# Moving the expert stage's residual sums and the last gate conversions in a one-core transformer block

## The chip, the cores and the metric

The kernel runs on one core of one Trainium2 chip. The metric is device time in microseconds (us) of one execution. Four compute engines work from queues of their own: PE (TensorE: matrix products, with PEld as its weight loads), DVE (VectorE), ACT (ScalarE) and POOL (GpSimd); SP issues most of the DMA transfers. An instruction runs when those ahead of it in its engine's queue have run and the semaphores that it waits for have come.

## The reference, cut to what matters

All tensors are float32; there are 1024 tokens of 1024 channels, 32 experts, four experts per token.

```python
h = layer_norm(DEEPNORM_ALPHA * h + mix, ln1_g, ln1_b)         # first half of the block: attention, gating
logits = h @ w_router + b_router                               # top 4 of 32 experts per token
gate = min(xb @ w_gate + b_gate, 7); up = clip(xb @ w_up + b_up, -7, 7)
y = ((up + 1) * gate * sigmoid(1.702 * gate)) @ w_down + b_down    # per expert, for its tokens
h = layer_norm(DEEPNORM_ALPHA * h + sum_of_gated_y, ln2_g, ln2_b)
ple = (p @ w_ple) * sigmoid(h @ w_ple_gate + b_ple_gate)
out = layer_norm(DEEPNORM_ALPHA * h + ple, ln3_g, ln3_b)
```

## The kernel before, in words

Precision is kept with pairs of float16: a float32 weight or activation is split into a high part (an ACT copy, scaled) and a low part (a DVE scalar_tensor_tensor that subtracts the high part), and a product takes three matmuls (high by high, high by low, low by high). A piece of weight of 512 rows by 512 columns is a "unit". `stage` loads it (1 MB, SP queue), `high(n)` makes its high part on ACT and `low(n)` its low part on DVE; `convert(n)` is both.

The instructions of each engine are issued in the order in which the Python program writes them (`tc.manual_schedule()`). Small `Pipe` objects delay work by a number of ticks: `p.at(2, f)` runs f two ticks later, so the place of a `tick` or a `drain` decides where in each queue an instruction stands. Operations that a pipe runs directly carry the line of `Pipe.tick`, L63.

The expert stage (`moe`) walks through `seq`, a list of steps numbered n, one unit each. Per expert (r, in the order ORDER) these are eight steps for the gate and up products ("g" and "u") and four for the down product ("d"). At step n the program runs `high(n + 4)`, then `low(n + 3)`, then the step's matmuls. For the first expert, steps 0 to 7 are the g and u products, steps 8 to 11 the d product; this expert is one of three in FULL, whose down weights are not split but used as float32 straight from the stage, so those four units have no conversion. Step 12 begins the second expert (window 96 tokens), step 20 the third (window 232).

Around this stand four things that the change touches:

- The tiles' sums. `start(i)` in `mid` (L888) multiplies tile i's gates by the 32 down biases (two matmuls, L895, into two PSUM banks of the eight that all of PE's work shares), adds ALPHA times the residual (two DVE operations on 128x512, L63, one tick later) and writes the 512 KB tile to `acc` in device memory (POOL queue, two ticks later). There are eight tiles. `step()` (L990) ticks mid's pipe and starts one tile; it is called at the end of each step n below 14 (L1534), so that the tiles start at steps 0 to 7. Expert results are later added to `acc` by indirect transfers (L1379), whose order behind those writes is kept.
- `find(2, pipe)` (L1525), at step 4: a one-hot mask on DVE (eight operations, L1240) for the third expert; two ticks later PE picks the tokens (L1248), and a tick after that POOL gathers their rows (L1267).
- The gate of the last part, `w_ple_gate`, is four units, converted as numbers len(seq) to len(seq)+3. The first is converted within the last d product, the second right after the steps (L1542), ahead of a hardware loop over overflowing tokens (`For_i`, L1548), the last two behind it in `more()` (L1595). Of the 16 `ple_tile` products (six matmuls each, evicted by ACT), eight are before the loop and eight behind it. With these inputs the loop is passed without a turn.
- The last part (`post`): three tiles of `acc` are loaded, `more()` runs, tile 0 is normalised on DVE and transposed by `turn` (PE, then a split on ACT and DVE), and tile 1 is normalised. Then the loop over eight tiles runs `gate(i, 0)`, which ends in a matmul with the bias row `k.bg` (L1697; the row is split by `fill_bg`, on ACT and DVE), `turn(i + 1)` and `gate(i, 1)`. `gate(i, 0)` reads units 0 and 1, `gate(i, 1)` units 2 and 3.

Of the kernel before, what the change touches and what calls it, by code (L numbers as in the profile page):

```python
# [205 lines left out]
def three(nc, ps, n, lhs, rhs):  # L206

    for b in range(n):
        (lh, ll), (rh, rl) = lhs(b), rhs(b)
        nc.tensor.matmul(ps, lh, rh, start=b == 0, stop=False)  # L210
        nc.tensor.matmul(ps, lh, rl, start=False, stop=False)  # L211
        nc.tensor.matmul(ps, ll, rh, start=False, stop=b == n - 1)  # L212
# [19 lines left out]
def pair(t, *sl):  # L232
    return lambda b: tuple(t[(slice(None), s, b, *sl)] for s in range(2))
# [908 lines left out]
def moe(k, windows, m, p):  # L1142
# [5 lines left out]
    R = len(windows)  # L1148
# [6 lines left out]
    pipe = Pipe()  # L1155
# [22 lines left out]
    seq = []  # L1178
# [14 lines left out]
    staged, units, seen = {}, {}, set()  # L1193
# [12 lines left out]
    def high(n):  # L1206
        if n < len(loads):
            if loads[n][0] == "p" or loads[n][0] == "d" and full(loads[n][1]):
                units[loads[n]] = staged.pop(n)
                return  # L1210
            units[loads[n]] = k.t8([P, 2, KB // 2, 512], F16, "unit")
            nc.scalar.activation(units[loads[n]][:, 0], staged[n], AF.Copy, scale=WS)  # L1212

    def low(n, part=None):

        if 0 <= n < len(loads):
            if n in staged:
                u = units[loads[n]]
                sl = slice(0, 4) if part is None else slice(2 * part, 2 * part + 2)
                nc.vector.scalar_tensor_tensor(u[:, 1, sl], staged[n][:, sl], WS, u[:, 0, sl], op0=OP.mult, op1=OP.subtract)  # L1220
                if part == 0:
                    return
                del staged[n]
            stage(n + N_AHEAD)

    def convert(n):
        high(n)
        low(n)
# [42 lines left out]
    def find(r, p, soon=False):  # L1271

        if r >= R:
            return
        oh = onehot(r, lambda b: k.place[:, b, r:r + 1])

        def second():
            ts = pick(r, oh, lambda b: k.val[:, b, :, r])
            if soon:
                gather(r, ts)  # L1280
            else:
                p.at(1, gather, r, ts)
        p.at(1 if soon else 2, second)

    def turn(r, w0, n, h, p):

        if r not in xgT:
            xgT[r] = k.t8([P, 2, KB, 256], F16, "xgT")
        t, x = xgT[r], xg[r, w0]
        pt = k.bank()  # L1290
        for j in range(4):
            b = 4 * h + j
            nc.tensor.transpose(pt[:, j * P:j * P + n], x[:n, b * P:(b + 1) * P], k.identf[:n, :n])
        src = pt.rearrange("p (j t) -> p j t", j=4)[:, :, :n]
        hi, lo = (t[:, s, 4 * h:4 * h + 4, w0:w0 + n] for s in range(2))

        def fin():
            nc.scalar.activation(hi, src, AF.Copy, scale=16.0)  # L1298
            nc.vector.scalar_tensor_tensor(lo, src, 16.0, hi, op0=OP.mult, op1=OP.subtract)  # L1299
        p.at(1, fin)  # L1300
# [26 lines left out]
    def s1(kind, r, u, p):  # L1327
        un = units.pop((kind, r, u))
        banks = chunks(kind, r, u)
        columns(r, u, un, xgT[r], banks)  # L1330
        if u % 2:
            p.at(1, take, kind, r, u // 2, banks, p)
# [98 lines left out]
    def ple_turns():  # L1431
        st = units.pop(("p", R, 0)).rearrange("p a (b c) -> p (a b) c", b=2)
        ple["p"] = k.t8([P, 2, 2, T], F16, "pT")
        for i in range(0, NB, 2):
            pt = k.bank()
            for j in range(4):
                nc.tensor.transpose(pt[:, j * P:(j + 1) * P], st[:, i + j // 2, (j % 2) * P:(j % 2 + 1) * P], k.identf)
            pt = pt.rearrange("p (i k t) -> p k i t", i=2, k=2)
            sl = slice(i * P, (i + 2) * P)
            hi, lo = (ple["p"][:, s, :, sl].rearrange("p k (i t) -> p k i t", i=2) for s in range(2))  # L1440

            def fin(hi=hi, lo=lo, pt=pt):
                for kk in range(2):
                    k.split(hi[:, kk], lo[:, kk], pt[:, kk], 16.0)
            pipe.at(1, fin)

    def ple_tile(i, h):
        if i % 2 == 0 and h == 0:
            ple[i] = k.t8([P, 2, D], FT, "ple")
            k.pl += [ple[i][:, 0], ple[i][:, 1]]  # L1450
        ps = k.bank()
        u = units["x", R, 0]
        three(nc, ps, 2, pair(ple["p"], slice(i * P, (i + 1) * P)), lambda b: tuple(u[:, s, 2 * b + h] for s in range(2)))
        pipe.at(1, nc.scalar.activation, k.pl[i][:, h * 512:(h + 1) * 512], ps, AF.Copy, 0.0, 1.0 / (16.0 * WS))

    k.pl = []
    ple_tiles = [(i, h) for i in range(NB) for h in range(2)]
# [27 lines left out]
    for n, (kind, r, u) in enumerate(seq):  # L1485
        pipe.tick()
        if n + LEAD < len(seq):
            high(n + LEAD)
        if n == 2:
            low(4)  # L1490
        if n > 1 and n + LEAD - 1 < len(seq):
            low(n + LEAD - 1)
        elif n == 0:
            low(2)
        if n >= 30:
            next(over, None)
        if n == len(seq) - 8:
            fill_bg = post_rows(k)
        if kind == "p":
            ple_turns()  # L1500
        elif kind == "d":
            if (r, u) == (R - 1, 1):
                for _ in range(2):
                    ple_tile(*ple_tiles.pop(0))
            if r in (0, R - 1) and u == 1:
                pipe.drain()
            if (r, u) == (R - 1, 1):
                convert(len(seq))
            s2(r, u, pipe)
            if r == 0 and u in (1, 3):  # L1510
                turn(1, 0, windows[1], u // 2, pipe)
        elif kind != "x":
            s1(kind, r, u, pipe)
            if n == 0:
                rest, turns, step, biases = next(m)
            if n == 1:
                biases("g", 0)
                turns()
                find(1, pipe, True)
                gather(0, pick(0, oh, val), False)  # L1520
                over = rest()
                low(3)
            if n in (3, 5, 7):
                biases(kind, u // 2)
            if n == 4:  # L1525
                find(2, pipe)
            if r and (kind, u) == ("g", 2):
                find(r + 2, pipe)
            if r and u >= 2 and r + 1 < R:
                i = 2 * (kind == "u") + u - 2  # L1530
                ws = win(r + 1)
                if i % 2 < len(ws):
                    turn(r + 1, *ws[i % 2], i // 2, pipe)
        if n < 14:  # L1534
            step()
        if n == 14:
            p.drain()
    for _ in range(3):
        pipe.tick()
        for _ in range(2):  # L1540
            ple_tile(*ple_tiles.pop(0))
    convert(len(seq) + 1)  # L1542
    pipe.drain()


# [1 line left out]
    n = nc.values_load(k.n_over[0:1, 0:1], min_val=0, max_val=N_OVER)  # L1547
# [43 lines left out]
    us = []  # L1591

    def more():

        for n in range(2, 4):  # L1595
            convert(len(seq) + n)
        us.extend(units.pop(("w", R, u)) for u in range(4))
        fill_bg()
        for n, t in enumerate(ple_tiles):
            ple_tile(*t)  # L1600
            if n % 2:
                pipe.tick()
        pipe.drain()
        del units["x", R, 0]
    return us, more


LEAD, N_AHEAD, N_FIRST = 4, 6, (4, 8)
# [3 lines left out]
def post_rows(k):  # L1612

    k.bg, fill = row_halves(k, k.a["b_ple_gate"], "bg")
    k.rows = {}
    for n in ("ln2_g", "ln2_b", "ln3_g", "ln3_b"):
        k.rows[n] = k.t4([P, D], FT, n)
        k.row(k.rows[n], k.a[n][0])
    return fill


def post(k, us, more, p):
# [10 lines left out]
    su, me, sq, va, y, t = (k.small([P, 2], FT, f"pn{c}", 1) for c in range(6))  # L1633
# [42 lines left out]
    def turn(i, h):  # L1676
        if h == 0:
            hs[i] = k.t4([P, 2, KB, P], F16, "h2T")
        pt = k.bank()
        for j in range(4):  # L1680
            b = 4 * h + j
            nc.tensor.transpose(pt[:, j * P:(j + 1) * P], h2[i][:, b * P:(b + 1) * P], k.identf)
        pt = pt.rearrange("p (j t) -> p j t", j=4)
        k.split(hs[i][:, 0, 4 * h:4 * h + 4], hs[i][:, 1, 4 * h:4 * h + 4], pt, 4.0)
# [24 lines left out]
    load(0)  # L1709
    load(1)  # L1710
    load(2)
    more()
    for i in range(2):
        k.norm(h2[i], D, rows["ln2_g"], rows["ln2_b"], EPS * AS * AS, None, 1 if i else 2)
        if i == 0:
            for h in range(2):
                turn(i, h)
    fin, done = None, {}

    def finish(i):  # L1720
# [76 lines left out]
```

## Time and profile before

| | us |
|---|---|
| three timed runs | 2163.43, 2163.64, 2168.16 (median 2163.64) |
| the profiled execution | 2162.48 |
| its span, first to last instruction | 2160.8 |
| PE, DVE, ACT busy | 2088.8, 1665.1, 1332.7 |

The profile has one execution. Besides totals it has timelines (start and duration of each instruction, and in brackets the idle time of the engine before it with what ended that), waits (who waited for whom) and windows (busy time by engine in a stretch, with the clock that TensorE was granted as a share of full speed). A PE matmul's duration is longer than its pitch, since matmuls are pipelined. Times below are counted from the span's start.

### The profile page before, as it was taken

Reading aid. Unit: us, or ns where it says so; the run is one execution under the profiler, and the core shown is the slowest. Engines: PE = TensorE matmul, PEld = TensorE weight load, DVE = VectorE, ACT = ScalarE, POOL = GpSimd, SP = SyncE. Lnnn points to the kernel's source line nnn. Section 1 sums busy time; section 2 is a strip of 40 time slices with the busy share of each in tenths; the row PEclk is TensorE's granted clock in tenths of the full one; section 3 lists DMA queues with packets and bytes.
Section 4 is the critical chain, followed back from the end, with each engine's and each line's share of the span. In section 5 each row is a group of like instructions: output and inputs, shape, how many; then the busy total and the mean of one; then the engine's idle time right before and its main releaser. Section 6 shows DMA issues by size and latency. Waiting matters only on the chain. (4 is left out here: it accounts for less than half of the span.)

```text
span 2160.8 us, 54807 instructions
## 1 busy us (share of the span) xinstructions
PE 2088.8 (97%) x23236; PEld 1695.0 (78%) x23236; DVE 1665.1 (77%) x2807; ACT 1332.7 (62%) x1925; POOL 262.4 (12%) x272
## 2 busy tenths in 40 slices
PE   7999889999999999999999999999999999999897
PEld 6797556544469879889889898999999989999443
DVE  4677666523256888969788899999889998998688
ACT  3324555412110357778778788888878888888642
POOL 1000000000100020111102121221312122221100
PEclk9999999999999999999999999999999999999999
DMA  7201211412132598999989999999999999999611
GB/s 249 70 21 31 72 51 56 127 45 63 50 113 79 220 340 307 347 354 355 368 301 336 347 361 375 364 347 366 354 319 367 359 361 346 363 348 377 212 49 59
DMA packets 278603, 520.14 MB, mean 241 GB/s; under 512 B 12092, under 2 KB 61292, under 8 KB 278320
## 3 DMA queue, kind: packets, MB, share of 16 engines
q1 hardware_dynamic: 262688, 464.10, 59.7%
q0 software_dynamic: 15664, 52.47, 9.0%
q8 instruction: 185, 3.03, 0.6%
q14 instruction: 66, 0.54, 0.1%
HBM read 476.93 MB, written 33.30 MB: 236 GB/s over the span
## 5 line engine op out<-in xcount | busy, mean ns | idle before, releaser
L1220 DVE SCALAR_TENSOR_TENSOR unit<-stage,unit 128x2048 f16<-128x2048 f32 (+1 forms) x378 | 856.8, 2278 | 73.3 <-ACT unit L1212 72.5
L1324 PE MATMUL bank<-xgT,unit 128*128 128x120 f16 (+22 forms) x4096 | 754.5, 226 | 1.2 <-DVE xgT L1299 1.2
L1323 PE MATMUL bank<-xgT,unit 128*128 128x120 f16 (+22 forms) x4096 | 754.7, 226 | 1.0 <-ACT z L1342 1.0
L1325 PE MATMUL bank<-xgT,unit 128*128 128x120 f16 (+22 forms) x4096 | 754.4, 226 | 0.7 <-DVE unit L1220 0.7
L1212 ACT ACTIVATE unit<-stage 128x2048 f16<-128x2048 f32 x377 | 717.0, 1912 | 49.3 <-DVE unit L1220 25.3
L1324 PEld LDWEIGHTS <-unit 128*128 128x128 f16 x5056 | 496.3, 98 | 7.1 <-issue 1.9
L1323 PEld LDWEIGHTS <-unit 128*128 128x128 f16 x5056 | 496.6, 98 | 6.2 <-issue 1.3
L1325 PEld LDWEIGHTS <-unit 128*128 128x128 f16 x5056 | 496.3, 98 | 4.8 <-issue 1.4
L1342 ACT ACTIVATE z<-bank,bias 128x120 f32<-128x120 f32 (+22 forms) x512 | 156.5, 379 | 88.3 <-PE bank L1325 87.8
L1323 PE MATMUL bank<-hT,unit 128*128 128x232 f16 (+14 forms) x960 | 207.8, 238 | 0.0
L1325 PE MATMUL bank<-hT,unit 128*128 128x232 f16 (+14 forms) x960 | 207.8, 238 | 0.0
L1324 PE MATMUL bank<-hT,unit 128*128 128x232 f16 (+14 forms) x960 | 207.8, 238 | 0.0
L1379 POOL DMA_INDIRECT acc_dram<-y,slot_i x47 | 117.3, 2495 | 527.8 <-ACT y L1376 523.8
L1267 POOL DMA_INDIRECT xg<-h_dram,slot_i x46 | 108.3, 2355 | 599.8 <-DVE slot_g L1262 314.3
L224 PE MATMUL bank<-xT,unit 128*128 128x512 f16 x384 | 145.5, 379 | 2.7 <-DVE pT L63 2.7
L226 PE MATMUL bank<-xT,unit 128*128 128x512 f16 x384 | 145.5, 379 | 1.6 <-DVE unit L105 1.6
L225 PE MATMUL bank<-xT,unit 128*128 128x512 f16 x384 | 145.5, 379 | 0.0
L210 PE MATMUL bank<-unit,xT 128*128 128x256 f16 (+1 forms) x384 | 106.2, 277 | 2.3 <-ACT unit L104 2.3
L211 PE MATMUL bank<-unit,xT 128*128 128x256 f16 (+1 forms) x384 | 106.0, 276 | 2.1 <-DVE unit L105 2.1
L212 PE MATMUL bank<-unit,xT 128*128 128x256 f16 (+1 forms) x384 | 106.0, 276 | 0.0
L105 DVE SCALAR_TENSOR_TENSOR unit<-stage,unit 128x1024 f16<-128x1024 f32 (+2 forms) x37 | 60.1, 1657 | 58.7 <-ACT unit L104 58.6
L1299 DVE SCALAR_TENSOR_TENSOR xgT<-bank,xgT 128x512 f16<-128x512 f32 (+7 forms) x92 | 50.7, 552 | 56.8 <-ACT xgT L1298 56.3
(392 smaller groups left out, 3499.1 us busy)
## 6 DMA issues: line engine op xcount, KB each, us to landing
stage<-in_w_gate_up_dram SPq DMA_DIRECT2D x256, 1024.0 KB, 9.7
stage<-in_w_down_dram SPq DMA_DIRECT2D x128, 1024.0 KB, 9.6
stage<-in_w_in_dram SPq DMA_DIRECT2D x22, 512.0 KB, 4.2
stack<-qk_tmp SPq DMA_DIRECT2D x96, 64.0 KB, 2.0
stage<-in_w_in_dram SPq DMA_DIRECT2D x5, 1024.0 KB, 11.3
xs<-in_x_dram SPq DMA_DIRECT2D x8, 512.0 KB, 12.2
crow<-c_dram SPq DMA_DIRECT2D x8, 512.0 KB, 4.5
stage<-in_w_out_dram SPq DMA_DIRECT2D x4, 1024.0 KB, 6.2
```

The lines of the kernel that those rows point to most:

```text
L210: nc.tensor.matmul(ps, lh, rh, start=b == 0, stop=False)
L224: nc.tensor.matmul(box[0], lh, rh, start=b == 0, stop=False)
L225: nc.tensor.matmul(box[0], lh, rl, start=False, stop=False)
L226: nc.tensor.matmul(box[0], ll, rh, start=False, stop=b == n - 1)
L1212: nc.scalar.activation(units[loads[n]][:, 0], staged[n], AF.Copy, scale=WS)
L1220: nc.vector.scalar_tensor_tensor(u[:, 1, sl], staged[n][:, sl], WS, u[:, 0, sl], op0=OP.mult, op1=OP.subtract)
L1267: nc.gpsimd.indirect_dma_start(out=x[:n], out_offset=None, in_=k.h1d, in_offset=bass.IndirectOffsetOnAxis(ap=i[:n, :1], axis=0))
L1323: nc.tensor.matmul(o, wh, x[:, 0, kb, :W], start=start, stop=False, skip_group_check=True)
L1324: nc.tensor.matmul(o, wh, x[:, 1, kb, :W], start=False, stop=False, skip_group_check=True)
L1325: nc.tensor.matmul(o, wl, x[:, 0, kb, :W], start=False, stop=stop, skip_group_check=True)
L1342: nc.scalar.activation(zs[r][c // 2][:, k0 + c % 2, :W], banks[c // n][:, c % n, :W], AF.Identity, bias=bias_of(r, 4 * v + c + 4 * k0), sc ...
L1379: st = nc.gpsimd.indirect_dma_start(out=k.acc, out_offset=bass.IndirectOffsetOnAxis(ap=idx[r, w0][:n, :1], axis=0), in_=y[:n], in_offset=N ...
```

## The change

The tiles' sums are started two per step in steps 8 to 11, and mid's pipe is drained at step 11 in place of step 14; `find(2)` stands at step 6 in place of step 4. The second gate unit is converted behind the loop in place of ahead of it. `more` becomes a generator of two parts: the first converts the second unit and runs the eight remaining `ple_tile`s (a tick after each, in place of after two); the second converts the last two units and the bias row. The first part is called where `more()` was, the second after tile 0 was normalised and transposed.

```diff
-            if n == 4:
+            if n == 6:
                 find(2, pipe)
...
-        if n < 14:
+        if 8 <= n < 12:
             step()
-        if n == 14:
+            step()
+        if n == 11:
             p.drain()
...
-    convert(len(seq) + 1)
     pipe.drain()
...
     def more():

+        convert(len(seq) + 1)
+        for t in ple_tiles:
+            ple_tile(*t)
+            pipe.tick()
+        pipe.drain()
+        del units["x", R, 0]
+        yield
         for n in range(2, 4):
             convert(len(seq) + n)
         us.extend(units.pop(("w", R, u)) for u in range(4))
         fill_bg()
-        for n, t in enumerate(ple_tiles):
-            ple_tile(*t)
-            if n % 2:
-                pipe.tick()
-        pipe.drain()
-        del units["x", R, 0]
-    return us, more
+        yield
+    return us, more()
...
-    more()
+    next(more)
     for i in range(2):
         k.norm(h2[i], D, rows["ln2_g"], rows["ln2_b"], EPS * AS * AS, None, 1 if i else 2)
         if i == 0:
             for h in range(2):
                 turn(i, h)
+            next(more)
```

## Rows read from the trace of the kernel before

**Rows 1.** The page: busy time, share of the span and instructions of each engine.
```profile
PE 2088.8 (97%) x23236; PEld 1695.0 (78%) x23236; DVE 1665.1 (77%) x2807; ACT 1332.7 (62%) x1925; POOL 262.4 (12%) x272
```
**Rows 2.** Windows, steps 1-7, 8-11, 12-20: busy us by engine, granted clock, DMA share, GB/s.
```profile
755.70:788.50 32.80, 30.23 (x421) 27.21 (x419) 27.52 (x61) 12.39 (x24) 11.01 (x10) 0.90 0.86 313
788.50:804.70 16.20, 16.20 (x77) 7.87 (x76) 10.88 (x14) 11.55 (x15) 1.20 (x3) 1.00 1.04 386
804.70:828.20 23.50, 22.38 (x427) 21.99 (x424) 23.40 (x33) 22.80 (x35) 2.15 (x2) 1.00 1.05 381
```
**Rows 3.** Groups by line, DVE, 755.7 to 788.5: busy us, mean ns, idle.
```profile
L63 DVE SCALAR_TENSOR_TENSOR h<-h,bank 128x512 f32<-128x512 f32 x14 | 8.9, 677 | 0.0
```
**Rows 4.** Timeline of DVE, steps 2 to 15.
```profile
765.10 4.48 DVE L1220 SCALAR_TENSOR_TENSOR unit<-stage,unit 128x2048 f16<-128x2048 f32 x2
...
788.55 1.28 DVE L63 SCALAR_TENSOR_TENSOR h<-h,bank 128x512 f32<-128x512 f32 x2 [2.78 <-PE bank L895]
...
794.64 2.28 DVE L1220 SCALAR_TENSOR_TENSOR unit<-stage,unit 128x2048 f16<-128x2048 f32 x1
796.84 0.40 DVE L1361 SCALAR_TENSOR_TENSOR hT<-sig,z 128x240 f32<-128x240 f32 x1
...
804.68 11.09 DVE L1220 SCALAR_TENSOR_TENSOR unit<-stage,unit 128x2048 f16<-128x2048 f32 x5
```
**Rows 5.** Waits of PE, 750 to 810: who for whom, us, times, longest.
```profile
PE bank L1248 <- DVE z L1359: 1.1, 1, 1.1
PE bank L1323 <- ACT z L1342: 1.0, 1, 1.0
...
PE bank L895 <- DVE h L63: 0.5, 1, 0.5
```
**Rows 6.** Windows of steps 4 and 5 alone (48 matmuls of a unit in each).
```profile
769.50:773.70 4.20, 4.20 (x49) 4.14 (x48) 4.20 (x6) 1.55 (x2) 2.08 (x3) 0.59 1.05 409
774.00:776.60 2.60, 2.60 (x50) 2.50 (x48) 2.60 (x4) 0.00 (x0) 0.53 (x1) 1.00 0.99 255
```
**Rows 7.** Tile view, steps 8 to 11: ns min/median/max, first and last start.
```profile
L1401 PE MATMUL bank<-stage,hT x32: 590/592/690, 788.6 to 802.5; 128*120 128x512 f32 x32
```
**Rows 8.** Timeline of DVE behind the loop.
```profile
2034.77 4.49 DVE L1220 SCALAR_TENSOR_TENSOR unit<-stage,unit 128x2048 f16<-128x2048 f32 x2
2039.28 1.22 DVE L701 SCALAR_TENSOR_TENSOR bg<-brow,bg 1x1024 f16<-1x1024 f32 x1
...
2052.36 1.29 DVE L105 SCALAR_TENSOR_TENSOR h2T<-bank,h2T 128x512 f16<-128x512 f32 x2 [5.17 <-ACT h2T L104]
2053.56 1.27 DVE L148 BATCH_NORM_STATS2 bn_s<-h 128x6 f32<-128x512 f32 x2
```
**Rows 9.** Timeline of ACT behind the loop.
```profile
2032.83 3.71 ACT L1212 ACTIVATE unit<-stage 128x2048 f16<-128x2048 f32 x2 [1.73 <-DVEq L1548]
...
2051.73 1.08 ACT L104 ACTIVATE h2T<-bank 128x512 f16<-128x512 f32 x2
```
**Rows 10.** Timeline of PE behind the loop.
```profile
2035.71 0.61 PE L210 MATMUL bank<-unit,pT 128*128 128x512 f16 x1 [5.44 <-DMA h<-acc_dram]
...
2039.83 0.58 PE L210 MATMUL bank<-unit,pT 128*128 128x512 f16 x1 [2.65 <-issue]
...
2057.86 0.38 PE L1697 MATMUL bank<-bg,sel 128*128 128x512 f16 x1
2059.91 1.09 PE L1682 MATMUL bank<-identf,h 128*128 128x128 f32 x8 [1.67 <-DVE pn L1645]
```
**Rows 11.** Line L1548 (the loop), 2015 to 2045: ns min/median/max, first and last start.
```profile
L1548 PEldq COMPARE_BRANCH  x3: 97/192/3594, 2028.2 to 2035.5; - x3
```
**Rows 12.** Waits of SP's queue, 2022 to 2110.
```profile
SPq L1548 <- DVEq L1548: 1.6, 1, 1.6
```
**Rows 13.** Windows behind the loop and in the last part.
```profile
2039.80:2042.90 3.10, 3.07 (x8) 1.12 (x8) 2.91 (x8) 0.60 (x1) 0.00 (x0) 0.50 0.49 197
2043.10:2051.00 7.90, 7.90 (x38) 3.62 (x37) 3.85 (x9) 3.58 (x6) 0.00 (x0) 1.00 0.00 0
...
2071.80:2139.00 67.20, 67.20 (x336) 33.41 (x335) 60.73 (x164) 29.54 (x54) 2.79 (x5) 1.00 0.15 55
```

## The prediction

> **What bounds the kernel now.** The page's totals come first: PE is busy for 97% of the span, DVE for 77% [rows 1]. Those are averages, so I read windows next, around the two places that the diff touches. In steps 1 to 7 (755.7 to 788.5) DVE has 27.5 of 32.8 us and PE's granted clock averages 0.90; in steps 8 to 11 PE is never idle and DVE has 10.9 of 16.2; from 804.7 to 828.2 DVE has 23.4 of 23.5 [rows 2]. So in this order the bound is DVE, then PE on float32 matmuls, then DVE. Behind the loop the chain of waits runs along PE: PE restarts at 2035.71, runs the eight remaining `ple_tile`s, and DVE waits 5.17 us for it before the split of tile 0 at 2052.36 [rows 8, 10]. In the last part PE is busy throughout (67.20 of 67.20 us) [rows 13], so what delays PE there delays the end.
>
> **Steps 0 to 7 get shorter.** 14 DVE operations of the sums, 8.9 us, lie in 755.7 to 788.5 [rows 3]; the last of the eight pairs is the one at 788.55, 1.28 us [rows 4]. All eight move. On PE that takes away:
> - the waits of 1.1, 1.0 and 0.5 us [rows 5], 2.6 us in all. I put them down to banks: two per tile, held until DVE, which lags, has read them, out of eight.
> - two slow steps. Step 4, behind the 1.0 us wait, ran at a granted clock of 0.59 (between the levels 1.2 and 2.4 GHz) and took 4.2 us; step 5, at 1.00, took 2.6 [rows 6]. Step 6, behind the 1.1 us wait, is like step 4. 2 x 1.6 = 3.2 us.
> - 16 matmuls (L895) at a pitch of 0.22 us: 3.5 us. The pitch is that of a 512-column matmul, 7.90 us by 38 at full clock, 0.21 [rows 13].
> - the pick of `find(2)`, 16 small matmuls, taken as 0.7 us (between nothing and the 1.1 us of the wait ahead of it); it comes back in step 8, so its size cancels.
>
> That is 10.0 us. About 0.9 of it comes back, because PE then catches up with DVE's low part of unit 3. Step 8 starts some 9 us earlier: 788.6 becomes 779.5. The conversions have room for that: two low parts take 4.48 us, from 765.10 [rows 4], with 3.7 us of sums gone ahead of the last of them.
>
> **Steps 8 to 11 take it back.** PE: 16 float32 products in 32 passes from 788.6 to 803.1 with half a microsecond of transposes between [rows 7], so 3.5 us per step, plus 0.9 for two tiles, plus 0.7 once. That alone would be 19 us, to 798.5. DVE doesn't let it. Its queue at step 8 holds the first pair of sums, which waits for the first tile's matmuls, which PE issues behind the step's own: 779.5 + 0.7 + 3.5 + 0.4 = 784.1. Until then DVE is idle and everything else queues behind. From there it has the 10.9 us of today less today's last pair (1.2), eight pairs at 8.9/7 = 1.27, and a microsecond for `find(2)`'s slots: 20.9, of which successive operations overlap by a tenth or two each, so about 20 us [rows 2 to 4]. PE's third float32 unit (step 10) needs the last hT. DVE reaches it after: first pair 1.2, slots and glu 1.4, low part 2.2, two pairs 2.4, glu 1.0, low part 2.2, hT 0.4: 794.9. Today the same hT runs at 796.84, when step 8 began at 788.6 [rows 4, 7]: it ended 8.7 us behind step 8's start and will end 15.4 behind it. PE wants it for step 10 at 788.8 and stands for some 4 us; 1.0 us was enough for a fall of the clock [rows 6], so I charge another 1.6. DVE in turn waits for tile 4's matmuls (1.4 us, and the 1.6 of the slow clock). The second expert's five low parts, which start at 804.68 [rows 4], then start at 784.1 + 20 + 1.4 = 805.5 without the clock's fall and at 807.1 with it. DVE has no slack from there to 828 [rows 2], so this passes on: +0.8 or +2.4 us. I take +2.4, since the shorter wait of rows 5 already cost it, and keep +0.8; at most 4.7 us could be gained (PE's 798.5 against 803.2).
>
> The queues in passing: POOL's eight writes to `acc` (512 KB each) go from steps 2 to 8 to steps 9 to 12, and the first indirect add waits for their landing; behind it in POOL's queue stands only the gather for the fourth expert, which step 16 asks for. SP's weight loads keep their order; the 4 MB of writes fall in a stretch in which the DMA share is 1.04 as well as 0.86 before it [rows 2], so loads up to step 17 come earlier and those after at the same time. I cost both at nothing; the cover is the order of megabytes, not spare rate, and if loads come late it costs up to 2 us. `find(2)`'s gather comes two steps later for a transpose at step 16: nothing.
>
> **Behind the loop.** The second unit's conversion leaves the place ahead of the loop. SP waited 1.6 us there for DVE [rows 12], so SP, ACT and DVE pass the loop up to 1.5 us earlier. PE does not: its branch took 3.594 us [rows 11], begun just after its last matmul, which the 5.44 us of idle put at 2030.3 [rows 10], and the restart at 2035.71 follows from that. The waits name the load of `acc` as the releaser of that restart [rows 10]; by them PE would start 1.5 us earlier too. The Trainium skill (Runtime: NRT & Kernel Launch, Instruction fetch mechanics) says that a taken branch to code outside the fetched window stalls until that code is fetched. By that rule the restart stays; by the waits the total below would be 1.5 us less.
>
> The unit itself, 1.9 us on ACT and 2.2 on DVE (half of the pairs of 3.71 and 4.49) [rows 8, 9], is hidden by PE's restart and `ple_tile`s, which end at 2051.0; the cover is over 9 us. The ticks change nothing, as ACT follows PE tile by tile.
>
> The last two units and the bias row ran in that same cover. Now they stand behind tile 0's split in both queues. ACT ends the split at 2052.8 (2051.73 + 1.08) [rows 9]; its first high part is there at 2054.6. DVE has then 4.49 + 1.22 [rows 8]: 2060.3, where before it went on at 2053.56 with tile 1's statistics [rows 8]. From those to the transposes of tile 1 at 2059.91 [rows 10] is 6.35 us. So the transposes start at 2066.65: +6.7 us. PE, which waited 1.67 us there [rows 10], has nothing else: `gate(0, 0)` ends in the bias row's matmul (2057.86 [rows 10]), now held to 2060.3, then 6.3 us of idle. After an idle time of 5.44 us PE ran at a granted clock of 0.50 [rows 10, 13]; half of 3.1 us is 1.6 lost. Between nothing and 2 us, I take 1.6.
>
> **Sum.** +2.4 + 6.7 + 1.6 = +10.7 us on the profiled execution's 2162.5: 2173.2. The median of the runs shown is 1.2 us above that execution, within its spread. Forecast: 2173 us, about 0.45% slower; its own range is 2170 to 2177 (head from 0 to +4, clock from 0 to 2).
>
> **Rivals.** About 0.3%, 6.5 us, is what can be told from no change: below 2157.1 is faster, above 2170.1 slower.
> 1. The head's gain stays (0.17). DVE keeps up in steps 8 to 11, and PE's own 19 us decide: -4.7 + 8.3 = +3.6, 2166 us, within. For it: DVE is a third idle there today. Against: the first pair is held behind the step's matmuls.
> 2. The other side, not slower: the last two conversions don't stand behind tile 0's split (0.08). Place: DVE's and ACT's queues between 2042 and 2052, where DVE has 10 us of idle. If low parts start before the split there, both tail terms go: +2.4, 2165 us, within; it decides once they start before 2051. Against: DVE stood 5.17 us before that split with tile 1's statistics behind it [rows 8], so its queue isn't reordered.
> 3. Both 1 and 2, with the 1.5 us of the loop (0.09): 2162.5 - 4.7 - 1.5 = 2156, faster.
> 4. The change doesn't do in steps 0 to 7 what it says (0.16): the waits of rows 5 come from ACT's and DVE's reads of other tiles and stay with their slow steps, 2 x (1.0 + 1.6) = 5.2, while four tiles' banks in each of steps 8 to 11 make new ones: 2178 us, slower.
>
> The forecast itself has 0.50. Slower: 0.50 + 0.16 + 0.04 of 1 = 0.70. Within: 0.13 of 1 + 0.08 of 2 = 0.21. Faster: 0.09. The range 2165 to 2179 leaves out rival 3 and the far end of 4.
>
> **What would show it.** Right: step 8 starting near 780; DVE idle until the first sums near 784; a PE stall of 3 to 5 us ahead of the third float32 unit; the second expert's low parts starting 0 to 3 us later than 804.68. Behind the loop PE restarting at the same distance from its last matmul, DVE's two low parts behind the split of tile 0, and an idle time of some 6 us ahead of tile 1's transposes with a half-clock stretch after it. Wrong: transposes of tile 1 within 2 us of today's place counted from PE's restart, or steps 12 on starting 3 us earlier.

## The result, and the profile after

The changed kernel takes 2176.32 us (median of 6 runs, 2173.99 to 2177.88) where the kernel before takes 2164.10 beside it: ratio 1.0052, 95% interval 1.0040 to 1.0064. It is slower by 12.2 us by the medians and by 11.3 by the ratio (8.7 to 13.9); 2173 was forecast, and the time lies in the range.

The page of the changed kernel, busy time by engine, hardly differs from [rows 1]: PE's busy time has grown by 5.9 us with the same number of matmuls, so some of them took longer; the rows below show some at half clock.

```profile
PE 2094.7 (96%) x23236; PEld 1697.0 (78%) x23236; DVE 1665.0 (77%) x2807; ACT 1333.3 (61%) x1925; POOL 271.3 (12%) x272
```

**A zero for the comparison.** Two profiled executions are not aligned before the changed code begins: the DVE operation at L910, just ahead of step 0, starts at 748.40 before and at 749.95 after. Places in the expert stage are therefore counted from that operation, places behind the loop from PE's restart there. A time "on the scale of before" is one of the changed kernel less those 1.55 us.

**The expert stage.** Windows of steps 1 to 7, 8 to 11 and 12 to 20 of the changed kernel (columns as in [rows 2]):

```profile
757.30:781.70 24.40, 24.03 (x382) 23.19 (x378) 18.03 (x39) 12.07 (x23) 9.72 (x1) 0.93 0.85 296
781.70:808.80 27.10, 22.90 (x123) 11.20 (x123) 20.28 (x36) 14.07 (x17) 7.11 (x10) 0.94 0.98 354
808.80:832.40 23.60, 22.25 (x408) 21.56 (x408) 23.50 (x33) 20.74 (x34) 3.26 (x4) 1.00 1.04 368
```

The first stretch shrank from 32.8 to 24.4 us. The second grew from 16.2 to 27.1, and in it PE, never idle before, is idle for 4.2. DVE shows why (timeline of the changed kernel; in brackets the idle time ahead and its releaser):

```profile
776.92 0.40 DVE L1361 SCALAR_TENSOR_TENSOR hT<-sig,z 128x240 f32<-128x240 f32 x1
782.18 0.16 DVE L1250 COPY slot_t<-bank 128x4 f32<-128x4 f32 x1 [4.86 <-PE bank L1248]
...
786.33 1.29 DVE L63 SCALAR_TENSOR_TENSOR h<-h,bank 128x512 f32<-128x512 f32 x2 [3.59 <-PE bank L895]
...
794.38 0.40 DVE L1361 SCALAR_TENSOR_TENSOR hT<-sig,z 128x240 f32<-128x240 f32 x1
...
796.90 0.40 DVE L1361 SCALAR_TENSOR_TENSOR hT<-sig,z 128x240 f32<-128x240 f32 x1
...
800.87 1.28 DVE L63 SCALAR_TENSOR_TENSOR h<-h,bank 128x512 f32<-128x512 f32 x2 [2.38 <-PE bank L895]
...
804.74 3.67 DVE L63 SCALAR_TENSOR_TENSOR h<-h,bank 128x512 f32<-128x512 f32 x6
```

DVE idles for 8.5 us in two waits at the pick and the first sums, 4.86 and 3.59, and again for 2.38; what queues behind the sums, the last two of hT's four pieces (L1361) among it, hardly gains. The last piece comes at 796.90, on the scale of before 1.5 us earlier than the 796.84 of [rows 4], though step 8 began 8.4 us earlier. PE's side of it, the pick of `find(2)`, then the first three of the four float32 products of steps 8 to 11 with the sums' matmuls behind the first two:

```profile
781.78 0.75 PE L1248 MATMUL bank<-val,oh 128*128 128x4 f16 x16
782.40 3.67 PE L1401 MATMUL bank<-stage,hT 128*120 128x512 f32 x8
785.91 1.03 PE L895 MATMUL bank<-bds,gst 96*128 96x512 f16 x4
786.77 3.60 PE L1401 MATMUL bank<-stage,hT 128*120 128x512 f32 x8
790.21 1.03 PE L895 MATMUL bank<-bds,gst 96*128 96x512 f16 x4
794.83 5.46 PE L1401 MATMUL bank<-stage,hT 128*120 128x512 f32 x8 [3.60 <-DVE hT L1361]
```

The third product waits 3.60 us for the third piece of hT (794.38 + 0.40) and then takes 5.46 us instead of 3.60: PE's granted clock is 0.67 in 794.8 to 798.0 and 0.50 in 798.0 to 799.0. Its second half reads the last piece, which is there at 797.30, as that half begins (797.4).

**Behind the loop.** DVE (L148 is the first operation of tile 1's norm), then PE:

```profile
2057.25 1.29 DVE L105 SCALAR_TENSOR_TENSOR h2T<-bank,h2T 128x512 f16<-128x512 f32 x2 [9.67 <-ACT h2T L104]
2059.53 4.49 DVE L1220 SCALAR_TENSOR_TENSOR unit<-stage,unit 128x2048 f16<-128x2048 f32 x2 [1.00 <-ACT unit L1212]
2064.06 1.22 DVE L701 SCALAR_TENSOR_TENSOR bg<-brow,bg 1x1024 f16<-1x1024 f32 x1
2065.30 1.29 DVE L148 BATCH_NORM_STATS2 bn_s<-h 128x6 f32<-128x512 f32 x2
```

```profile
2040.00 0.61 PE L210 MATMUL bank<-unit,pT 128*128 128x512 f16 x1 [5.57 <-DMA h<-acc_dram]
...
2044.36 0.58 PE L211 MATMUL bank<-unit,pT 128*128 128x512 f16 x1 [2.47 <-issue]
...
2055.93 1.04 PE L1684 MATMUL bank<-identf,h 128*128 128x128 f32 x8
2057.27 0.39 PE L1696 MATMUL bank<-unit,h2T 128*128 128x512 f16 x1 [0.30 <-ACT h2T L104]
...
2065.32 0.38 PE L1699 MATMUL bank<-bg,sel 128*128 128x512 f16 x1 [2.41 <-DVE bg L701]
2071.67 1.97 PE L1684 MATMUL bank<-identf,h 128*128 128x128 f32 x8 [5.96 <-DVE pn L1647]
```

Against [rows 8, 10] the reader sees two low parts and the bias row between tile 0's split and tile 1's norm, DVE idle for 9.67 us ahead of them, and PE idle for 2.41 and 5.96 behind them. The same places in all kernels run, as distances worked out from the timelines: "low parts" is the start of the second expert's row of low parts and "loop end" the end of PE's last matmul ahead of the loop, both from DVE's L910; turn 0, 1 and 2 are the starts of the transposes of tiles 0, 1 and 2 (for tile 0 of its first half, where the halves are apart), from PE's restart.

| kernel | low parts | loop end | turn 0 | turn 1 | turn 2 |
|---|---|---|---|---|---|
| before | 56.28 | 1281.88 | 15.33 | 24.20 | 35.92 |
| after | 58.85 | 1284.48 | 15.93 | 31.67 | 45.45 |
| head_only | 59.58 | 1285.49 | 15.71 | 24.59 | 36.31 |
| steps_first | 53.72 | 1279.32 | 15.25 | 24.12 | 35.84 |
| starts_4_7 | 52.13 | 1280.34 | 15.13 | 24.01 | 35.73 |
| tail_only | 57.25 | 1282.84 | 15.68 | 31.42 | 44.90 |
| unit1_past | 57.04 | 1282.64 | 15.34 | 24.22 | 35.93 |
| conv_ahead | 56.80 | 1283.11 | 30.05 | 40.26 | 51.99 |
| conv_after4 | 56.77 | 1282.51 | 25.59 | 35.80 | 47.52 |
| after_filled | 59.00 | 1284.87 | 15.69 | 32.16 | 43.83 |
| tile_in_gap | 56.89 | 1282.47 | 12.53 | 22.17 | 33.83 |
| steps_first_gap | 53.49 | 1279.12 | 12.31 | 21.94 | 33.61 |
| starts_4_7_gap | 52.14 | 1279.49 | 12.01 | 21.65 | 33.31 |

Six of these have the expert stage of before: their loop end has a mean of 1282.58 and lies within 0.7 of it. The three with that of the change (after, head_only, after_filled) have 1284.95. So the expert stage costs 2.4 us. Behind the restart the change costs 45.45 - 35.92 = 9.5.

### The profile page after: what moved, and what is told of

Read it like the earlier page. It is cut to its first block, busy times and chain, and to the rows that moved or that the text cites. A ratio compares the mean times of both kernels' runs of the same rounds, so it can differ in the third digit from the quotient of the medians.

```text
span 2174.6 us, 54812 instructions
## 1 busy us (share of the span) xinstructions
PE 2094.7 (96%) x23236; PEld 1697.0 (78%) x23236; DVE 1665.0 (77%) x2807; ACT 1333.3 (61%) x1925; POOL 271.3 (12%) x272
## 5 line engine op out<-in xcount | busy, mean ns | idle before, releaser
L1267 POOL DMA_INDIRECT xg<-h_dram,slot_i x46 | 117.4, 2552 | 597.1 <-DVE slot_g L1262 300.2
```

Of the source, the lines that this page charges most:

```text
L1267: nc.gpsimd.indirect_dma_start(out=x[:n], out_offset=None, in_=k.h1d, in_offset=bass.IndirectOffsetOnAxis(ap=i[:n, :1], axis=0))
```

## The experiments

**The two halves, each alone.** head_only:

```diff
-            if n == 4:
+            if n == 6:
                 find(2, pipe)
...
-        if n < 14:
+        if 8 <= n < 12:
             step()
-        if n == 14:
+            step()
+        if n == 11:
             p.drain()
```

> The expert stage's half of the change alone: pairs of sums in steps 8 to 11, the barrier at step 11, the pick of the third expert at step 6; everything behind the loop as before. Theory (the pairs of sums lengthen VectorE's row in steps 8 to 11 and the second expert's low parts end later): step 8 starts some 7 to 8 us earlier than before, the low parts that stood at 804.68 some 2.5 us later, and that carries through to the end: 2166.5 us where before is 2164, ratio 1.0012 (1.0006 to 1.002). Rival (the head's gain is kept, the change's loss is all behind the loop): 2158 to 2162 us. Second rival (the head's half carries all of the loss, by way of what the expert stage leaves to the end): 2176 us.

Measured: 2168.21 us against 2164.22, ratio 1.0014 (1.0005 to 1.0023). Low parts and loop end are 2.7 and 2.9 us later than the means of the six. The theory's +2.5 holds; both rivals lie outside the interval.

tail_only is the rest of the diff (unit 1 in the first part of `more`, units 2 and 3 and the bias row in the second, called behind tile 0's `turn`).

> The half behind the loop alone: the gate's units 1 to 3 and the bias row past the loop, units 2 and 3 behind tile 0's transposes, the four tiles of embeddings ahead; the expert stage as before. Theory (VectorE has the conversions behind tile 0's split, so tile 1's transposes come some 6.9 us later, and the clock's low stretch is some 2 us dearer): about 9 us slower than before, 2173 us, ratio 1.0042 (1.003 to 1.005), with tile 1's eight transposes some 11 us later against the last matmul of the loop's stretch than TensorE had them, less what the restart moves. Rival (no loss here, all of it comes from the expert stage): 2164 us, ratio 1.000.

Measured: 2174.75 us, ratio 1.0045 (1.0032 to 1.0059), +9.7 us by the ratio. Turn 1 is 7.2 us later than in the kernel before and turn 2 9.0. (The "11 us" of the expectation was a slip: it is the distance of the two traces' raw times, 2071.67 - 2059.91 = 11.8, which holds the shift of the whole run as well.) The two halves add up to the change within the intervals, 1.4 + 4.5 = 5.9 thousandths against 5.2 (4.0 to 6.4); an interaction smaller than that isn't excluded.

**The expert stage: the order inside a step.** steps_first has head_only's steps, barrier and place of `find(2)`, but issues the two tiles' matmuls ahead of the step's product:

```diff
             if (r, u) == (R - 1, 1):
                 convert(len(seq))
+            if r == 0:
+                step()
+                step()
             s2(r, u, pipe)
...
-        if n < 14:
-            step()
-        if n == 14:
+        if n == 11:
             p.drain()
```

> The expert stage's half of the change, but in each of steps 8 to 11 the two tiles' matmuls are issued ahead of the step's own product; behind the loop as before. Theory (in the changed kernel the first pair of sums waits at the head of VectorE's row for matmuls that stand behind 16 float32 matmuls, and the 3.6 us for which TensorE waits for hT and the late low parts follow from that): VectorE's first pair of sums comes about 1 us behind the start of step 8 instead of 4, its idle stretch shrinks from 3.6 to under 1 us, TensorE waits less than 1 us for hT, and the five low parts start some 3 us earlier than in the change's own order, level with before or up to 1 us ahead of it: 2163 us, ratio 0.9990 to 1.0003. Rival (the low parts are held by the sum of VectorE's work in these steps, whatever its order): as the half alone measured, 2167 us, ratio 1.0014.

Measured: 2161.26 us, ratio 0.9978 (0.9969 to 0.9987): faster than before by 4.8 us by the ratio. The chain went as the theory says (timeline of DVE):

```profile
781.86 0.16 DVE L1250 COPY slot_t<-bank 128x4 f32<-128x4 f32 x1 [4.85 <-PE bank L1248]
782.25 0.16 DVE L1250 COPY slot_t<-bank 104x4 f32<-104x4 f32 x1 [0.23 <-PE bank L1248]
782.49 1.28 DVE L63 SCALAR_TENSOR_TENSOR h<-h,bank 128x512 f32<-128x512 f32 x2
...
790.54 0.40 DVE L1361 SCALAR_TENSOR_TENSOR hT<-sig,z 128x240 f32<-128x240 f32 x1
...
793.06 0.40 DVE L1361 SCALAR_TENSOR_TENSOR hT<-sig,z 128x240 f32<-128x240 f32 x1
...
803.36 11.09 DVE L1220 SCALAR_TENSOR_TENSOR unit<-stage,unit 128x2048 f16<-128x2048 f32 x5
```

DVE has the same operations as in the change, without the waits of 3.59 and 2.38 us. The wait of 4.85 us at the pick is still there, so it isn't what costs. hT's last two pieces come at 790.54 and 793.06, PE's list of waits no longer names hT (its third product takes 3.96 us), and the low parts come 5.4 us earlier than in the changed kernels' mean of 59.14. The gain was larger than expected: the low parts are 3.1 us ahead of before, not up to 1. The rival, that DVE's sum of work decides whatever its order, falls.

starts_4_7 puts the same eight starts two per step into steps 4 to 7, with `find(2)` at step 6 and the barrier at step 8:

```diff
-            if n == 4:
+            if n == 6:
                 find(2, pipe)
...
-        if n < 14:
+        if 4 <= n < 8:
             step()
-        if n == 14:
+            step()
+        if n == 8:
             p.drain()
```

> Two tiles' sums start in each of steps 4 to 7 instead of one in each of steps 0 to 7 (before) or two in each of steps 8 to 11 (the change); the barrier at step 8, the pick of the third expert at step 6, behind the loop as before. Theory (steps 0 to 3 gain some 4 us from having no sums, and steps 8 to 11 stay free of them, so VectorE has its conversions done in time): the five low parts start some 2 to 3 us earlier than before, 2161.5 us, ratio 0.9980 to 0.9995. Rival (VectorE carries 8 pairs in 4 steps of 3.5 us beside the first expert's gate stage, so its row grows by what steps 0 to 3 gained): 2164 us, ratio 1.000; if the sums also hold up hT as in the change, 2167 us.

Measured: 2160.94 us, ratio 0.9978 (0.9968 to 0.9988). The theory's direction holds, and the low parts are further ahead than expected: 4.7 us earlier than the mean of before. Not all of it arrives. The fifth low part waits for ACT, a wait that before does not have there ("x5" in [rows 4], "x4" here), and the loop's end is 2.2 us earlier only:

```profile
801.97 8.89 DVE L1220 SCALAR_TENSOR_TENSOR unit<-stage,unit 128x2048 f16<-128x2048 f32 x4
...
813.17 2.29 DVE L1220 SCALAR_TENSOR_TENSOR unit<-stage,unit 128x2048 f16<-128x2048 f32 x1 [2.31 <-ACT unit L1212]
```

By the ratio the gain is 4.8 us (2.6 to 6.9). The trace shows 2.2 at the loop's end and 0.2 behind it; where the rest lies is not shown.

**Behind the loop: which place costs.** unit1_past moves unit 1 alone past the loop:

```diff
-    convert(len(seq) + 1)
     pipe.drain()
...
-        for n in range(2, 4):
+        for n in range(1, 4):
             convert(len(seq) + n)
```

> One edit: the gate's unit 1 is converted behind the loop with units 2 and 3 instead of at the loop's end; all else as before. Theory (ScalarE and VectorE have room ahead of the second norm, so that this place is hidden): within 1 us of before, 2164, ratio 0.9995 to 1.0005. Rival (ahead of the norms each conversion delays h2's split and tile 0's transposes by its whole length, 1.9 us on ScalarE and 2.3 us on VectorE): 2166 us, ratio 1.001.

Measured: 2164.49 us, ratio 1.0003 (0.9994 to 1.0012). The interval doesn't exclude the rival's 1.001; the trace does, as turn 0 and turn 1 stand within 0.02 us of before. Hidden, as costed: DVE does all three low parts in one go and still waits 3.25 us for tile 0 (5.17 in [rows 8]).

```profile
2036.05 6.70 DVE L1220 SCALAR_TENSOR_TENSOR unit<-stage,unit 128x2048 f16<-128x2048 f32 x3 [3.05 <-ACT unit L1212]
2042.76 1.22 DVE L701 SCALAR_TENSOR_TENSOR bg<-brow,bg 1x1024 f16<-1x1024 f32 x1
...
2053.93 1.29 DVE L105 SCALAR_TENSOR_TENSOR h2T<-bank,h2T 128x512 f16<-128x512 f32 x2 [3.25 <-ACT h2T L104]
```

conv_ahead is tail_only with the second part called right behind the first, so ahead of both norms and of tile 0's split:

```diff
     next(more)
+    next(more)
     for i in range(2):
...
                 turn(i, h)
-            next(more)
```

> The half behind the loop once more, but with units 2 and 3 and the bias row converted ahead of the two norms and of tile 0's split, only behind the four tiles of embeddings. Theory (it is the place behind tile 0's split that costs, not the four tiles' earlier place and not that the first unit is converted past the loop): tile 1's transposes are back to within 1 us of where before has them, and the time within 1.5 us of before: 2164, ratio 0.9993 to 1.0007. Rival (the loss comes from putting the conversions past the loop's end at all, or from the tiles' transposes ahead of them on TensorE): 2171 to 2173 us.

Measured: 2181.17 us, ratio 1.0075 (1.0061 to 1.0088). The theory failed, and the rival's figure was too small as well: this place costs 16 us, more than the change's. ACT shows the reason (timeline):

```profile
2035.31 1.91 ACT L1212 ACTIVATE unit<-stage 128x2048 f16<-128x2048 f32 x1 [1.69 <-issue]
2043.59 0.60 ACT L63 ACTIVATE ple<-bank 128x512 f32<-128x512 f32 x1 [6.37 <-PE bank L212]
...
2054.91 0.60 ACT L63 ACTIVATE ple<-bank 128x512 f32<-128x512 f32 x1 [0.70 <-PE bank L212]
2055.41 3.70 ACT L1212 ACTIVATE unit<-stage 128x2048 f16<-128x2048 f32 x2
```

Each `ple_tile` is copied out of its bank by ACT once PE has done it (ACT waits 6.37 us for the first of them behind unit 1's conversion and 0.70 us for the last), and ACT's rows stand in the order of issue. Two conversions issued behind the eight tiles therefore start at 2055.41, when the last tile is out, and not at 2032.83 as in [rows 9]; the low parts follow at 2057.34 on DVE, and only behind them and the bias row, at 2063.08, does tile 0's norm begin, which before was done at 2047.2 (2052.36 - 5.17 in [rows 8]). PE stands still for 13.54 us. The cover of the conversions was PE's run of `ple_tile`s, and they lose it the moment they are issued behind these.

conv_after4 puts four of the eight tiles ahead of them and four behind:

```diff
-    convert(len(seq) + 1)
     pipe.drain()
...
-        for n in range(2, 4):
-            convert(len(seq) + n)
-        us.extend(units.pop(("w", R, u)) for u in range(4))
-        fill_bg()
+        convert(len(seq) + 1)
         for n, t in enumerate(ple_tiles):
+            if n == 4:
+                pipe.tick()
+                for m in range(2, 4):
+                    convert(len(seq) + m)
+                us.extend(units.pop(("w", R, u)) for u in range(4))
+                fill_bg()
             ple_tile(*t)
-            if n % 2:
-                pipe.tick()
+            pipe.tick()
```

> The conversions of units 2 and 3 and the bias row stand behind four of the eight half tiles of embeddings and ahead of the other four (unit 1 ahead of all); the norms and tile 0's split behind them as before. The version with all eight ahead took 2181 us, the one with none 2164. Theory (ScalarE's row: a conversion can't start before the evictions issued ahead of it, which wait for TensorE's half tiles, and VectorE's norm of tile 0 queues behind the conversions): each half tile ahead costs some 1.3 us, so the conversions start some 5 us earlier than behind all eight, 2175 to 2177 us, ratio 1.005 to 1.006. Rival (what cost 17 us was that TensorE ran dry and its clock fell, not the order on ScalarE: with four half tiles left to cover the conversions there is nothing to pay): 2164 to 2166 us, ratio 1.000 to 1.001.

Measured: 2175.97 us, ratio 1.0054 (1.0040 to 1.0067), as ACT's order has it. The conversions start 12.6 us behind PE's restart (17.1 behind all eight tiles), and turn 1 is 4.5 us earlier than in conv_ahead:

```profile
2048.70 0.60 ACT L63 ACTIVATE ple<-bank 128x512 f32<-128x512 f32 x1 [0.70 <-PE bank L212]
2049.19 3.70 ACT L1212 ACTIVATE unit<-stage 128x2048 f16<-128x2048 f32 x2
```

**The clock's share.** after_filled is the changed kernel with spare matmuls behind `gate(0, 0)`:

```diff
         f0 = gate(i, 0)
+        if i == 0:
+            spare = k.bank()
+            for b in range(24):
+                nc.tensor.matmul(spare, hs[0][:, 0, b % 8], us[0][:, 0, b % 4], start=b == 0, stop=b == 23)
```

> The changed kernel with 24 spare matmuls (128x128 by 512, their result is not read) on TensorE behind the first half gate of tile 0, in the stretch in which it waits for tile 1's norm; they fill about 5.2 of the 6 us of that wait. Theory (some 2 of the tail's 9 us are the half clock that follows the wait): tile 1's transposes start where the change has them, take 1.04 us instead of 2, and the gate behind them runs at the full clock at once: 1.5 to 2 us off the changed kernel, 2174.5 us, ratio to before 1.0045. Rival (the clock falls anyway behind the 2.4 us wait for the bias row, or the spare matmuls delay the transposes): 2176 to 2177 us, ratio 1.0052 to 1.006.

Measured: 2174.66 us, ratio 1.0043 (1.0029 to 1.0056); from the changed kernel's 1.0052 that is inside the intervals, so the trace decides. Windows, first of the changed kernel from tile 1's transposes on, then of after_filled: the spare matmuls, and the same stretch behind them (the column behind POOL's is the granted clock):

```profile
2071.70:2076.10 4.40, 4.40 (x15) 2.68 (x16) 1.57 (x3) 2.81 (x5) 0.00 (x0) 0.52 0.00 0
```

```profile
2065.40:2072.20 6.80, 6.80 (x25) 2.78 (x24) 5.66 (x16) 0.00 (x0) 0.00 (x0) 0.75 0.00 0
2072.20:2076.00 3.80, 3.80 (x23) 2.23 (x22) 1.70 (x3) 2.70 (x5) 0.00 (x0) 1.00 0.02 4
```

Turn 1 to turn 2 takes 11.67 us instead of 13.78, against 11.72 before: the half clock (1.2 GHz) behind the wait was 2.1 us of the loss. The rival was right in part. The clock had fallen behind the 2.41 us wait, so the spare matmuls took 6.8 us in place of 5.2 (the clock was 0.50 in 2067 to 2069) and turn 1 is 0.5 us later.

**A version that beats both.** tile_in_gap is the kernel before, with the last two of the eight `ple_tile`s behind tile 0's first half gate:

```diff
         for n, t in enumerate(ple_tiles):
+            if n == 6:
+                pipe.drain()
+                yield
             ple_tile(*t)
...
-    return us, more
+        yield
+    return us, more()
...
-    more()
+    next(more)
...
         f0 = gate(i, 0)
+        if i == 0:
+            next(more)
```

> The kernel before with one edit behind the loop: the last two of the eight half tiles of embeddings (12 matmuls, 2.6 us) are run behind tile 0's first half gate instead of ahead of tile 0's transposes. Theory (VectorE is what tile 1's transposes wait for, and it starts tile 1's norm from tile 0's split, which TensorE reaches 2.6 us earlier): tile 0's transposes 2.6 us earlier, the 1.7 us wait for tile 1's norm gone, all behind it 1.7 us earlier: 2162.5 us, ratio 0.9988 to 0.9997. Rival (tile 0's own norm is the limit, or the two tiles' evictions on ScalarE hold tile 1's split): 2164 us, ratio 1.000.

Measured: 2161.97 us, ratio 0.9986 (0.9977 to 0.9995). PE goes from one to the other without a wait:

```profile
2056.70 0.38 PE L1701 MATMUL bank<-bg,sel 128*128 128x512 f16 x1
2056.91 0.38 PE L210 MATMUL bank<-unit,pT 128*128 128x512 f16 x1
...
2059.29 0.38 PE L212 MATMUL bank<-unit,pT 128*128 128x512 f16 x1
2059.51 1.04 PE L1686 MATMUL bank<-identf,h 128*128 128x128 f32 x8
```

The 1.67 us of [rows 10] are gone, and turn 2 is 2.1 us earlier. Both versions of the expert stage together with this edit:

> The two versions that came out faster than before put together: the tiles' sums two per step in steps 4 to 7 (pick of the third expert at step 6), and the last two half tiles of embeddings behind tile 0's first half gate. Theory (the two gains lie in different stages, 4.5 us in the expert stage and 3.4 us by the medians behind the loop, where the trace shows 2.1): they add, 2158 to 2159 us, ratio 0.9965 to 0.9970. Rival (they share a limit behind the loop): 2161 us, ratio 0.9978.

> The same with the sums in steps 8 to 11 ahead of each step's own product, and the last two half tiles of embeddings behind tile 0's first half gate. Theory (gains add): 2158 to 2159 us, ratio 0.9965 to 0.9970. Rival (a shared limit behind the loop): 2161 us, ratio 0.9978.

Measured: 2160.26 us, ratio 0.9977 (0.9968 to 0.9986), and 2160.31 us, ratio 0.9978 (0.9969 to 0.9987). Each is some 5 us faster than before, and 16 us faster than the change. The ratios are those of the rival, and by them the second edit added nothing to the first. By the traces it did, as turn 2 is 2.4 us (starts_4_7_gap) and 2.2 us (steps_first_gap) earlier behind the restart, with the loop's end where it was or earlier; from L910 to the end of the span the traces are 2.6 and 2.2 us shorter. Half of either interval is 2 us, as much as the gain in question, and no run compares a version with the edit directly with one without, so whether the gains add stays open.

## Why the prediction was right, point by point

- **Steps 0 to 7 get shorter, by 8.4 us (9.1 forecast).** Step 8 begins with the pick's matmuls at 781.78 (above); that is 780.2 on the scale of before, where 779.5 was forecast. The banks' waits of [rows 5] and the slow steps of [rows 6] are gone, so rival 4, in which they stay, falls. Not foreseen was another slow stretch: PE now waits 0.37 us ahead of the small matmuls of `find(1)` at 760.58, and its clock is 0.65 on the mean from 760.5 to 764.9, where before had 1.00. Estimated from these figures it costs up to 1.5 us.
- **Steps 8 to 11 take it back, and 2.4 us more.** First sums at 784.8 on the scale of before (forecast 784.1), PE's stall 3.60 us (some 4), the product behind it 1.86 us slower (1.6 charged), low parts 2.3 us later in the mean (2.4 taken). The stall came near by luck: the prediction let step 10 wait for the last hT, and from its own 788.8 to 794.9 that is 6.1 us, not 4. In the trace step 10 starts on the third piece, 2.5 us ahead of the last, and the last was later than forecast (795.8 on the scale of before, against 794.9). steps_first shows the named cause, the sums at the head of DVE's row behind the step's float32 product: with only that order changed, the stage gains 3 us. Rival 1 was the right picture of that other order, not of this change.
- **PE's restart stays.** SP, which loads `acc`, no longer waited for DVE and took its branch 0.8 us behind PE's last matmul (2.3 before). A restart set by that load would have come 1.5 us earlier; PE's idle time is 5.57 us (5.44), with a branch of 3.727 us (3.594), and in steps_first, with 5.19 us, the profile names another releaser. So the load was not what set it. In all 13 kernels the idle time is PE's long branch (3.347 to 3.827 us) and 1.77 to 1.85 us, whatever releaser the profile names. The rule cited from the Trainium skill (Runtime: NRT & Kernel Launch, Instruction fetch mechanics) agrees with this; that the branch's time is a fetch, no run here shows.

The branches behind that point, of the changed kernel (columns as in [rows 11]); PE's is the long one:

```profile
L1548 PEldq COMPARE_BRANCH  x3: 97/193/3727, 2032.3 to 2039.7; - x3
...
L1548 SPq COMPARE_BRANCH  x2: 38/38/38, 2026.1 to 2035.2; - x2
```

- **Tile 1's transposes come 6.7 us later, with 1.6 us of half clock (forecast).** From turn 0 to turn 1 it is 15.74 against 8.87 us, +6.9; from turn 1 to turn 2 +2.1. Rivals 2 and 3 fall, since DVE's row stands as issued.
- **What was missing.** 0.6 us from the restart to turn 0: behind the same idle time the half clock lasted until 8.7 us past the restart, 7.2 before. This need not come from the change: head_only, whose code there is that of before, has 8.4 us of half clock and turn 0 at 15.71. With it 2.4 + 6.9 + 2.1 + 0.6 = 12.0 us, inside the interval of 8.7 to 13.9; the forecast had 10.7. Another 1.6 us of the distance from 2173 to 2176.3 is the base, the profiled execution's 2162.5 against a median of 2164.1.
- **Where the reason was too narrow.** The prediction laid the 6.7 us on the place behind tile 0's split. conv_ahead shows that the conversions are already exposed once they stand behind the `ple_tile`s in ACT's order; behind the split is, of the exposed places tried, the cheapest one: tile 0's gate still runs meanwhile, and PE idles for 2.41 and 5.96 us there, against 13.54 in conv_ahead.

## What to carry to other kernels

An operation is hidden by another engine's run only if no engine that it needs has an instruction ahead of it that waits for that run: look for its predecessors in each engine's order, not for its idle time. Work handed from PE to a second engine is to be issued on PE ahead of a long product if it stands first in the other's row; the same two calls, moved from behind the step's product to ahead of it, turned +3.0 us into -4.8 by the ratios. A wait that another engine's serial work sets can be filled by independent work from the stretch ahead of it, which also starts that serial work earlier.

## What the runs showed of the hardware that was not expected

The time at the lower clock behind much the same idle time differs: behind 5.3 to 5.6 us at the loop's end PE ran at half clock for 7.2 us before, 8.7 after, 8.4 in head_only and 9.3 in conv_ahead; behind conv_ahead's 13.54 us, for 3.4 us only. Rows of conv_ahead from the restart on and from tile 0's transposes on:

```profile
2038.30:2047.60 9.30, 6.95 (x16) 2.30 (x17) 1.25 (x1) 1.19 (x2) 0.00 (x0) 0.50 0.49 192
...
2068.40:2071.80 3.40, 2.97 (x11) 2.00 (x12) 2.16 (x4) 1.36 (x3) 0.00 (x0) 0.50 0.00 0
```

The first has a second pause in it, 2.29 us soon behind the restart (2.65 before, 2.47 after) with no releaser but "issue"; what PE does in it no run shows.
